# A streaming encoder step on one core: stationary tiles low in SBUF, and the up projection with tokens on partitions

## The chip, the cores and the metric

The kernel runs on one core of a Trainium2 chip. The metric is the device time of one execution in microseconds (us), less being better. The work is in float32, with every large product made of three products of a high and a low part.

## The reference

One layer of a hybrid encoder, for 256 prompt tokens and 8 x 16 sample tokens, 384 in all, with the same weights.

```python
h    = rmsnorm(x, norm_mix_g)                 # x: 384 tokens x 2048
proj = h @ w_in                               # GLU in | q | k | v | forget logits | gate A | gate B
u    = glu(proj); z = layernorm(causal_dwconv(u, 31 taps))
a    = swish(z) @ conv_pw_out
b    = forgetting_attention(q, k, v, logf, caches) @ w_att_out
x    = x + (sigmoid(gA) * a + sigmoid(gB) * b) @ w_out
h2   = rmsnorm(x, norm_ffn_g)
up   = h2 @ w_up                              # 2048 x 11264: gate half g, linear half u
gc   = causal_dwconv(g, 3 taps over time)     # per channel, per stream
x    = x + (silu(gc) * u) @ w_down            # 5632 x 2048
```

It returns x and the new caches and states (k, v, forget logits, conv rows, the last two gate rows).

## The kernel before

**Three products.** A weight block of 256 rows x 512 columns (two steps k of 128) arrives by one DMA of 512 KB as tile raw. ScalarE casts it to hi (line 144, type float32r), VectorE subtracts hi from raw to get lo (line 145). There are three raw buffers and two hi/lo pairs. Activations are kept as high and low parts too: tiles of 2 x 4 x 384 elements a partition (12,288 bytes), channels on partitions, tokens along the row. Each step k then takes three matmuls: high by high, high by low, low by high.

**Two kinds of job.** The function gemm runs jobs of nk steps. In kind "A" the weight block is stationary (128 x 128) and the 384 tokens move, lines 235 to 237; there are four blocks m, so 12 matmuls a step, and the result has channels on partitions. In kind "B" the activation is stationary (128 tokens at a time, three blocks t) and 512 weight columns move, lines 240 to 242; 9 matmuls a step, tokens on partitions. A job gathers in 4 or 3 of the five banks of the pool acc. At its last step evac empties each bank and done starts what follows. Before each pair of steps, ahead(2) gives out fetch and split of further weight pairs, until two are ready.

**Order.** PE, in parts SP, ScalarE and VectorE follow the order of the program; for the rest a planner works out, before the launch, the order on each engine from priorities (splits and evacuations are given out as if 150 and 60 instructions earlier) and from its own table of durations. after(n, f) runs f after n further steps.

**Stages.** V (columns 344 wide, kind B) with the first norm: first_norm transposes x by chunks on TensorE, x_chunk multiplies by the norm weight and splits into hT, lines 272 to 276. Then K, Q (B); GLU (A) beside attention; the gates (B, evacuated on ScalarE with a sigmoid, line 759) beside the 31-tap conv on VectorE; attention out with aHL and pointwise out with zt stationary (B, 8 steps each); w_out with mix (B). The second norm: x_chunk2 makes xg, second_norm gets 1/rms per token as a column, and diagonals and over_partitions (a product with ones, line 322) spread it as rs2 along the row of every partition. Then the feed-forward part: 11 groups of 512 channels, each with one up job for g and one for u (both A, 16 steps), and three rounds of down jobs (B, stationary act) after groups 4, 8 and 10.

In a group, up_g_evac multiplies PSUM by rs2 on VectorE into extf (line 939; 24 blocks of 16 tokens, each with two columns of left context, filled by POOL, lines 941 and 942). up_g_done runs the three taps on VectorE (956, 958), Silu on ScalarE (960) and sg = silu * rs2 on POOL (961). up_u_evac multiplies PSUM by sg (978) and splits into act (980, 981).

**Places in SBUF.** 229,376 bytes a partition are there. The lowest 16,384 are the descriptor scratch of POOL's DMAs. From the left follow the constants, raw, hi, lo, and five slots of 12,288 bytes for hT, mix, act and ut. From the right come attT, the conv tiles, attention's aHL, zt, the gates, and later y and xg. By the sizes of the tiles, in bytes from the start of a partition:

| tile | before | after |
|---|---|---|
| hi | 33,888 to 42,080 | 2,176 to 14,464 |
| lo | 42,080 to 50,272 | 211,968 to 224,256 |
| five act slots | 50,272 to 111,712 | 14,464 to 75,904 |
| aHL0, aHL1 | 178,432 to 203,008 | 75,904 to 100,480 |
| zt0 | 166,144 to 178,432 | 100,480 to 112,768 |
| zt1 | 217,056 to 229,344 | 112,768 to 125,056 |
| xg0 to xg3 | 178,592 to 227,744 | 75,904 to 125,056 |

Of the kernel before, what the change touches and what calls it, by code (L numbers as in the profile page):

```python
# [40 lines left out]
def hybrid_step(  # L41
# [20 lines left out]

    cp, close_cp = pool("consts")
    wp, close_wp = pool("weights")
    gp, close_gp = pool("acts")
# [58 lines left out]
    def stream_tile():  # L124
        return wp.tile([P, 2, 512], F32, tag="raw", bufs=3, name="raw")

# [90 lines left out]
    def gemm(jobs, sides=()):  # L217
        for js in jobs:
            js = js if isinstance(js, tuple) else (js,)
            for j in js:  # L220
                nb = 4 if j["kind"] == "A" else NTT
                j["ps"] = [(misc_tile if j is not js[0] and i == 2 else acc_tile)() for i in range(nb)]
            for j, k in [(j, k + i) for k in range(0, js[0]["nk"], 2) for j in js for i in range(2)]:
                nb, n, nk, ps = len(j["ps"]), j["n"], j["nk"], j["ps"]
                kk = k % 2
                if kk == 0:
                    ahead(2)
                    hi, lo = ready.pop(0)
                ah, al = j["act"](k)
                st, sp = k == 0, k == nk - 1  # L230
                for m in range(nb):
                    s = slice(m * P, (m + 1) * P)
                    if j["kind"] == "A":
                        o = ps[m][:, :NT]
                        mm(o, hi[:, kk, s], ah, start=st, stop=False)  # L235
                        mm(o, hi[:, kk, s], al, start=False, stop=False)  # L236
                        mm(o, lo[:, kk, s], ah, start=False, stop=sp)  # L237
                    else:
                        o = ps[m][:, :n]
                        mm(o, ah[:, s], hi[:, kk, :n], start=st, stop=False)  # L240
                        mm(o, ah[:, s], lo[:, kk, :n], start=False, stop=False)  # L241
                        mm(o, al[:, s], hi[:, kk, :n], start=False, stop=sp)  # L242
# [69 lines left out]

    def diagonals(p, r, tag):
        dg = p.tile([P, NTT, P], F32, tag=tag + "d", name=tag + "d")
# [61 lines left out]
    def first_norm():  # L376
        for c in range(2, 16, 2):
            yield
            x_chunk(c)
            yield  # L380
            x_chunk(c + 1)
            yield
            if c % 4 == 2:
# [13 lines left out]
        yield  # L397
        dg = diagonals(p_x0, rs1, "r1")
        yield
# [363 lines left out]
    def layer_norm():  # L763
# [24 lines left out]
        yield  # L788
        dg = diagonals(p_cv, rv, "rv")
        yield  # L790
# [3 lines left out]
        for c in range(8):  # L794
# [8 lines left out]
            yield  # L803

    zt = [p_z.tile([P, 2, 4, NT], F32R, name="zt0"), p_t.tile([P, 2, 4, NT], F32R, tag="T", name="zt1")]

# [47 lines left out]
    def open_resid():  # L854
        close_sg()
        close_z()
        close_hl()
        close_cv()
        close_t()
        p_r, res["close_r"] = pool("resid", side="right")  # L860
        res["y"] = y = p_r.tile([P, NTT, DM], F32, name="y")
        res["xg"] = [p_r.tile([P, 2, 4, NT], F32R, name=f"xg{g}") for g in range(4)]
        res["rs2"] = p_r.tile([P, NT], F32, name="rs2")
        res["ss2"] = p_r.tile([P, NTT, 4], F32, name="ss2")
# [34 lines left out]
    def second_norm():  # L899
# [15 lines left out]
    for u, i0 in enumerate(range(0, 11, 3)):  # L915
# [11 lines left out]
        after(2 + 2 * u, ffn_state)  # L927
    extf = [p_f.tile([P, 24, 18], F32, name=f"extf{m}") for m in range(4)]
    for m in range(4):
        nc.gpsimd.memset(extf[m][:, 0, 0:2], 0.0)  # L930
    xa = grouped(xg)
    acts = {}

    def up_g_evac(g, sg):
        def ev(m, ps):
            c = 4 * g + m
            e = extf[m]
            v = e[:, :, 2:18]
            tt(v, ps[:, :NT].rearrange("p (a t) -> p a t", t=16), rs2[:].rearrange("p (a t) -> p a t", t=16),
               op=ALU.mult)  # L940
            nc.gpsimd.tensor_copy(e[:, 1:16, 0:2], e[:, 0:15, 16:18])
            nc.gpsimd.tensor_copy(e[:, 16:24, 0:2], sfT[:, c, :].rearrange("p (b r) -> p b r", r=2))
        return ev

    def up_g_done(g, sg):
        def done():
            gcs = [p_f.tile([P, NT], F32, tag="gc", bufs=4, name="gc") for _ in range(4)]
            lc = p_f.tile([P, 18, 4], F32, tag="lc", bufs=2, name="lc")
            for w in range(3):
                for m in range(4):  # L950
                    c = 4 * g + m
                    o = gcs[m][:].rearrange("p (a t) -> p a t", t=16)
                    v = extf[m][:, :, w:w + 16]
                    wc = fw[:, w * 44 + c:w * 44 + c + 1]
# [4 lines left out]
            for m in range(4):  # L959
                nc.scalar.activation(gcs[m][:], gcs[m][:], AF.Silu)  # L960
                nc.gpsimd.tensor_tensor(sg[m][:], gcs[m][:], rs2[:], op=ALU.mult)
                nc.gpsimd.tensor_copy(lc[:, :, m].rearrange("p (a r) -> p a r", r=2), extf[m][:, 15:24, 16:18])

# [10 lines left out]

    def up_u_evac(g, sg):
        def ev(m, ps):
            a = p_f.tile([P, NT], F32, tag="ac", bufs=2, name="ac")
            tt(a[:], ps[:, :NT], sg[m][:], op=ALU.mult)
            hi, lo = acts[g][:, 0, m, :], acts[g][:, 1, m, :]
            nc.scalar.copy(hi, a[:])  # L980
            tt(lo, a[:], f(hi), op=ALU.subtract)
# [25 lines left out]
    close_f()  # L1007
    close_r()
    close_misc()
    close_acc()  # L1010
    close_gp()
    close_wp()
    close_cp()
    close_dr()
# [33 lines left out]
```

## Time and profile before

| what | value |
|---|---|
| median of 3 runs | 2037.92 us (2037.69 to 2038.57) |
| profiled execution, its own time | 2039.01 us |
| its span, first to last instruction | 2037.3 us |
| TensorE, busy | 2028.7 us |
| VectorE, busy | 1030.2 us |
| ScalarE, busy | 712.6 us |
| POOL, busy | 161.4 us |
| DMA | 276.12 MB, mean 136 GB/s |

A line of the groups reads: line, engine, operation, tiles written <- tiles read (the moving one ahead of the stationary one for matmuls), shape, count, then busy us in all, mean ns of one, and idle us of the engine just before, with what ended that idle time. Matmuls overlap in the pipeline, so their listed durations add up to more than the span. A timeline row begins with the start and the length in us. A row of the waits names who waited for whom, us in all, how often, and the longest. A row of the chain of waits has start, length and what ran.

### The profile page before, as it was taken

The page shows a single profiled execution, that of the slowest core. Times are in us where ns is not written, and L with a number is a line of the kernel's source. Part 1 is how long each engine was busy: PE and PEld are TensorE (multiplying, and loading weights), DVE is VectorE, ACT ScalarE, POOL GpSimd, SP SyncE. Part 2 cuts the span into 40 slices and gives each one's busy share as a digit, 9 for nine tenths or more (in the row PEclk, how much of TensorE's full clock was granted, in tenths as well). Part 3 has the DMA queues.
Part 4 walks back from the last instruction along what each step waited for, and adds up shares of the span by engine and source line. Part 5 has one row for each costly group of instructions (what it writes and reads, how often), then busy time and mean ns, then how long its engine had stood idle before and what let it go on. Part 6 is the DMA issues. An engine that isn't in the chain of part 4 may idle for free.

```text
span 2037.3 us, 26618 instructions
## 1 busy us (share of the span) xinstructions
PE 2028.7 (100%) x10668; PEld 1835.8 (90%) x10668; DVE 1030.2 (51%) x1416; ACT 712.6 (35%) x1034; POOL 161.4 (8%) x258
## 2 busy tenths in 40 slices
PE   9999999999999999999999999999999999999999
PEld 9988999988888888889999999889999998899987
DVE  4434477788753645344545354333544453335443
ACT  5444555433333523333323232322322332223322
POOL 2000011000000000000222022000221120002100
PEclk9999999999999999999999999999999999999999
DMA  6555555444444343643444444444444444444453
GB/s 181 170 169 158 152 169 152 117 133 134 134 129 130 121 123 118 193 124 114 125 127 124 134 125 125 133 125 132 128 124 125 130 130 125 130 128 126 128 152 124
DMA packets 175749, 276.12 MB, mean 136 GB/s; under 512 B 11998, under 2 KB 63217, under 8 KB 175617
## 3 DMA queue, kind: packets, MB, share of 16 engines
q1 hardware_dynamic: 175305, 273.84, 45.1%
q8 instruction: 83, 1.36, 0.3%
q0 software_dynamic: 288, 0.57, 0.2%
q14 instruction: 41, 0.34, 0.1%
q10 hardware_dynamic: 32, 0.01, 0.0%
HBM read 266.98 MB, written 7.86 MB: 135 GB/s over the span
## 4 chain that ended last, share of the span: by engine, by line
PE 98%; DVE 1%; DMA 0%; ACT 0%; issue 0%; SPq 0%; ACTq 0%; DVEq 0%
PE acc L241 17%; PE acc L242 17%; PE acc L240 17%; PE acc L235 14%; PE acc L236 14%; PE acc L237 14%; DMA xs<-in_x_sample_dram 0%; PE misc L559 0%; PE misc L885 0%; PE misc L838 0%; PE misc L272 0%; PE misc L625 0%; PE misc L592 0%; DVE lo L145 0%; PE misc L611 0%
## 5 line engine op out<-in xcount | busy, mean ns | idle before, releaser
L145 DVE TENSOR_TENSOR lo<-raw,hi 128x1024 fp32r<-128x1024 f32 (+2 forms) x481 | 585.2, 1217 | 907.5 <-ACT hi L144 902.3
L144 ACT CAST hi<-raw 128x1024 fp32r<-128x1024 f32 (+2 forms) x481 | 498.2, 1036 | 1169.1 <-PE acc L242 642.5
L235 PE MATMUL acc<-xg,hi 128*128 128x384 f32 x1408 | 474.9, 337 | 0.0
L237 PE MATMUL acc<-xg,lo 128*128 128x384 f32 x1408 | 473.1, 336 | 0.0
L236 PE MATMUL acc<-xg,hi 128*128 128x384 f32 x1408 | 473.1, 336 | 0.0
L240 PE MATMUL acc<-hi,hT 128*128 128x512 f32 (+1 forms) x704 | 267.6, 380 | 0.0
L241 PE MATMUL acc<-lo,hT 128*128 128x512 f32 (+1 forms) x704 | 265.3, 377 | 0.9 <-DVE lo L145 0.9
L235 PEld LDWEIGHTS acc<-xg,hi 128*128 128x128 f32 x1408 | 264.7, 188 | 1.4
L242 PE MATMUL acc<-hi,hT 128*128 128x512 f32 (+1 forms) x704 | 265.3, 377 | 0.0
L236 PEld LDWEIGHTS acc<-xg,hi 128*128 128x128 f32 x1408 | 264.8, 188 | 0.1
L237 PEld LDWEIGHTS acc<-xg,lo 128*128 128x128 f32 x1408 | 264.7, 188 | 0.0
L241 PE MATMUL acc<-lo,act 128*128 128x512 f32 x528 | 205.4, 389 | 0.0
L242 PE MATMUL acc<-hi,act 128*128 128x512 f32 x528 | 205.4, 389 | 0.0
L240 PE MATMUL acc<-hi,act 128*128 128x512 f32 x528 | 205.4, 389 | 0.0
L711 DVE SCALAR_TENSOR_TENSOR ut<-ext,cw,ut 128x384 f32<-128x384 f32 x240 | 152.1, 634 | 6.2
L241 PEld LDWEIGHTS acc<-lo,hT 128*128 128x128 f32 x704 | 132.5, 188 | 23.6 <-DVE lo L145 1.6
L240 PEld LDWEIGHTS acc<-hi,hT 128*128 128x128 f32 x704 | 132.5, 188 | 22.5 <-issue 0.2
L242 PEld LDWEIGHTS acc<-hi,hT 128*128 128x128 f32 x704 | 132.3, 188 | 22.6
L242 PEld LDWEIGHTS acc<-hi,act 128*128 128x128 f32 x528 | 99.1, 188 | 20.8
L241 PEld LDWEIGHTS acc<-lo,act 128*128 128x128 f32 x528 | 99.1, 188 | 20.4
L240 PEld LDWEIGHTS acc<-hi,act 128*128 128x128 f32 x528 | 99.1, 188 | 20.4
L235 PE MATMUL acc<-hT,hi 128*128 128x384 f32 x256 | 90.0, 352 | 0.0
(292 smaller groups left out, 1941.6 us busy)
## 6 DMA issues: line engine op xcount, KB each, us to landing
raw<-in_w_up_dram SPq DMA_DIRECT2D x176, 512.0 KB, 3.6
raw<-in_w_in_dram SPq DMA_DIRECT2D x96, 512.0 KB, 3.5
raw<-in_w_down_dram SPq DMA_DIRECT2D x88, 512.0 KB, 3.7
raw<-in_w_in_dram SPq DMA_DIRECT2D x64, 256.0 KB, 2.9
raw<-in_w_out_dram SPq DMA_DIRECT2D x32, 512.0 KB, 3.6
raw<-in_w_att_out_dram SPq DMA_DIRECT2D x16, 512.0 KB, 3.7
raw<-in_conv_pw_out_dram SPq DMA_DIRECT2D x16, 512.0 KB, 3.7
raw<-in_w_in_dram SPq DMA_DIRECT2D x23, 344.0 KB, 3.1
```

The lines of the kernel that those rows point to most:

```text
L144: nc.scalar.copy(hi[:, k, :o], raw[:, k, :o])
L145: tt(lo[:, k, :o], raw[:, k, :o], f(hi[:, k, :o]), op=ALU.subtract)
L235: mm(o, hi[:, kk, s], ah, start=st, stop=False)
L236: mm(o, hi[:, kk, s], al, start=False, stop=False)
L237: mm(o, lo[:, kk, s], ah, start=False, stop=sp)
L240: mm(o, ah[:, s], hi[:, kk, :n], start=st, stop=False)
L241: mm(o, ah[:, s], lo[:, kk, :n], start=False, stop=False)
L242: mm(o, al[:, s], hi[:, kk, :n], start=False, stop=sp)
L711: stt(o, v, wc, o, op0=ALU.mult, op1=ALU.add)
```

## The change

The constants, raw and lo go to the right side, hi to the bottom of the left; aHL, zt and xg go to the left behind the act slots; the descriptor scratch shrinks to 2,048 bytes. There are three hi/lo pairs and ahead(3). In first_norm each pair of chunks is turned one step later. The up jobs become kind B: ScalarE evacuates with the token's 1/rms as scale into tok (tokens on partitions), and VectorE turns it back by 16 transposes of 32 partitions x 384 elements a job, into extf or uT. The spread of rs2 goes, and POOL's product with it. The product of u with sg reads SBUF now.

```diff
-    cp, close_cp = pool("consts")
-    wp, close_wp = pool("weights")
+    cp, close_cp = pool("consts", side="right")
+    rp, close_rp = pool("raw_lo", side="right")
+    wp, close_wp = pool("hi")
...
-        return [wp.tile([P, 2, 512], F32R, tag=tag, bufs=2, name=tag) for tag in ("hi", "lo")]
+        return [p.tile([P, 2, 512], F32R, tag=tag, bufs=3, name=tag) for p, tag in ((wp, "hi"), (rp, "lo"))]
...
-                    ahead(2)
+                    ahead(3)
...
         for c in range(2, 16, 2):
             yield
+            yield
             x_chunk(c)
             yield
             x_chunk(c + 1)
-            yield
...
-    p_hl, close_hl = pool("attHL", side="right")
+    p_hl, close_hl = pool("attHL")
     aHL = [p_hl.tile([P, 2, 4, NT], F32R, name=f"aHL{i}") for i in range(2)]
-    p_z, close_z = pool("z", side="right")
+    zt = [p_hl.tile([P, 2, 4, NT], F32R, name=f"zt{i}") for i in range(2)]
...
+        p_xg, res["close_xg"] = pool("xg")
+        res["xg"] = [p_xg.tile([P, 2, 4, NT], F32R, name=f"xg{g}") for g in range(4)]
...
-        res["rs2"] = p_r.tile([P, NT], F32, name="rs2")
+        res["rs2"] = p_r.tile([P, NTT], F32, name="rs2")
...
-        dg = diagonals(p_f, r2, "r2")
-        after(2, lambda: over_partitions(dg, rs2[:]))
+        nc.vector.tensor_copy(rs2[:], r2[:])
...
-    def up_g_evac(g, sg):
-        def ev(m, ps):
-            c = 4 * g + m
-            e = extf[m]
-            v = e[:, :, 2:18]
-            tt(v, ps[:, :NT].rearrange("p (a t) -> p a t", t=16), rs2[:].rearrange("p (a t) -> p a t", t=16),
-               op=ALU.mult)
-            nc.gpsimd.tensor_copy(e[:, 1:16, 0:2], e[:, 0:15, 16:18])
-            nc.gpsimd.tensor_copy(e[:, 16:24, 0:2], sfT[:, c, :].rearrange("p (b r) -> p b r", r=2))
+    def tok_rows():
+        return p_f.tile([P, NTT, 512], F32, tag="tok", bufs=1, name="tok")
+
+    def up_evac(rows):
+        def ev(t, ps):
+            nc.scalar.activation(rows[:, t, :], ps[:], AF.Identity, scale=rs2[:, t:t + 1])
         return ev
 
-    def up_g_done(g, sg):
+    def blocks(rows, put):
+        src = rows[:].rearrange("p t (m b j) -> p b m t j", m=4, b=4)
+        for b in range(4):
+            for a in range(4):
+                nc.vector.transpose(put(a, slice(32 * b, 32 * b + 32)), src[32 * a:32 * a + 32, b])
+
+    def up_g_done(g, rows, sg):
         def done():
+            def put(a, js):
+                return extf[js].rearrange("p m (t a) c -> p m t a c", t=NTT)[:, :, :, 2 * a:2 * a + 2, 2:18]
+
+            blocks(rows, put)
...
             for m in range(4):
-                nc.scalar.activation(gcs[m][:], gcs[m][:], AF.Silu)
-                nc.gpsimd.tensor_tensor(sg[m][:], gcs[m][:], rs2[:], op=ALU.mult)
+                nc.scalar.activation(sg[m][:], gcs[m][:], AF.Silu)
...
-    def up_u_evac(g, sg):
-        def ev(m, ps):
-            a = p_f.tile([P, NT], F32, tag="ac", bufs=2, name="ac")
-            tt(a[:], ps[:, :NT], sg[m][:], op=ALU.mult)
-            hi, lo = acts[g][:, 0, m, :], acts[g][:, 1, m, :]
-            nc.scalar.copy(hi, a[:])
-            tt(lo, a[:], f(hi), op=ALU.subtract)
-        return ev
+    def up_u_done(g, rows, sg):
+        def done():
+            uT = p_f.tile([P, 4, NT], F32, tag="uT", bufs=1, name="uT")
+            blocks(rows, lambda a, js: uT[js].rearrange("p m (t a i) -> p m t a i", t=NTT, a=4)[:, :, :, a])
+            for m in range(4):
+                tt(uT[:, m], uT[:, m], sg[m][:], op=ALU.mult)
+                hi, lo = acts[g][:, 0, m, :], acts[g][:, 1, m, :]
+                nc.scalar.copy(hi, uT[:, m])
+                tt(lo, uT[:, m], f(hi), op=ALU.subtract)
+        return done
...
-        return [job("A", 16, xa, up_g_evac(g, sg), done=up_g_done(g, sg)), job("A", 16, xa, up_u_evac(g, sg))]
+        gr, ur = tok_rows(), tok_rows()
+        return [job("B", 16, xa, up_evac(gr), done=up_g_done(g, gr, sg)),
+                job("B", 16, xa, up_evac(ur), done=up_u_done(g, ur, sg))]
...
-    nc = _bacc.Bacc("TRN2", target_bir_lowering=False, num_devices=1)
+    nc = _bacc.Bacc("TRN2", target_bir_lowering=False, num_devices=1, dynamic_dma_scratch_size=2048)
```

More of the change, by code (lines that the diff above doesn't have):

```diff
@@ L124, in stream_tile @@
     def stream_tile():
-        return wp.tile([P, 2, 512], F32, tag="raw", bufs=3, name="raw")
+        return rp.tile([P, 2, 512], F32, tag="raw", bufs=3, name="raw")
     def fetch_row(raw, srcs, k):
@@ L311, in hybrid_step, with diagonals @@
     rs1b = cp.tile([P, NT], F32, name="rs1b")
-    def diagonals(p, r, tag):
-        dg = p.tile([P, NTT, P], F32, tag=tag + "d", name=tag + "d")
+    def diagonals(dg, r):
         for t in range(NTT):
@@ L397, in first_norm @@
         yield
-        dg = diagonals(p_x0, rs1, "r1")
+        dg = diagonals(p_x0.tile([P, NTT, P], F32, name="r1d"), rs1)
         yield
@@ L803, in layer_norm @@
             yield
-    zt = [p_z.tile([P, 2, 4, NT], F32R, name="zt0"), p_t.tile([P, 2, 4, NT], F32R, tag="T", name="zt1")]
     def conv_branch():
@@ L855, in open_resid @@
         close_sg()
-        close_z()
-        close_hl()
         close_cv()
         close_t()
+        close_hl()
+        p_xg, res["close_xg"] = pool("xg")
+        res["xg"] = [p_xg.tile([P, 2, 4, NT], F32R, name=f"xg{g}") for g in range(4)]
         p_r, res["close_r"] = pool("resid", side="right")
         res["y"] = y = p_r.tile([P, NTT, DM], F32, name="y")
-        res["xg"] = [p_r.tile([P, 2, 4, NT], F32R, name=f"xg{g}") for g in range(4)]
-        res["rs2"] = p_r.tile([P, NT], F32, name="rs2")
+        res["rs2"] = p_r.tile([P, NTT], F32, name="rs2")
         res["ss2"] = p_r.tile([P, NTT, 4], F32, name="ss2")
@@ L952, in done @@
                     o = gcs[m][:].rearrange("p (a t) -> p a t", t=16)
-                    v = extf[m][:, :, w:w + 16]
+                    v = extf[:, m, :, w:w + 16]
                     wc = fw[:, w * 44 + c:w * 44 + c + 1]
@@ L1008, in hybrid_step @@
     close_r()
+    res["close_xg"]()
     close_misc()
@@ L1012, in hybrid_step @@
     close_wp()
+    close_rp()
     close_cp()
```

14 lines of the change are left out of this document (9 added, 5 removed).

## The prediction

> **What bounds the kernel now.** I read the page first (busy times, the chain of waits, the groups), then single rows of the timeline, because a mean in the groups is the length of one pipelined matmul and not the distance to the next.
>
> ```profile
> span 2037.3 us, 26618 instructions
> PE 2028.7 (100%) x10668; PEld 1835.8 (90%) x10668; DVE 1030.2 (51%) x1416; ACT 712.6 (35%) x1034; POOL 161.4 (8%) x258
> PE 98%; DVE 1%; DMA 0%; ACT 0%; issue 0%; SPq 0%; ACTq 0%; DVEq 0%
> L235 PE MATMUL acc<-xg,hi 128*128 128x384 f32 x1408 | 474.9, 337 | 0.0
> L236 PE MATMUL acc<-xg,hi 128*128 128x384 f32 x1408 | 473.1, 336 | 0.0
> L237 PE MATMUL acc<-xg,lo 128*128 128x384 f32 x1408 | 473.1, 336 | 0.0
> ACT hi L144 <- PE acc L236: 473.9, 170, 3.5
> ```
>
> TensorE is busy for 2028.7 of 2037.3 us and holds 98% of the chain that ends last. ScalarE's casts wait for TensorE, not the other way round. So time is the sum over matmuls of the distance from one start to the next; a change pays only by fewer matmuls, a shorter distance, or fewer pauses. The up projection is 3 x 1408 = 4224 matmuls with 384 columns, of lines 235 to 237. Their listed 337 ns cannot be the distance: 4224 x 337 ns would be 1423 us of overlapping bars. The distances come from pairs of timeline rows. Between the first and the second row of each pair below lie 60 starts (30 for zt):
>
> ```profile
> 1009.90 0.34 PE L236 MATMUL acc<-xg,hi 128*128 128x384 f32 x1
> 1020.30 0.34 PE L236 MATMUL acc<-xg,hi 128*128 128x384 f32 x1
> 149.76 0.39 PE L240 MATMUL acc<-hi,hT 128*128 128x512 f32 x1
> 163.36 0.39 PE L240 MATMUL acc<-hi,hT 128*128 128x512 f32 x1
> 1289.97 0.39 PE L242 MATMUL acc<-hi,act 128*128 128x512 f32 x1
> 1303.57 0.39 PE L242 MATMUL acc<-hi,act 128*128 128x512 f32 x1
> 664.90 0.39 PE L240 MATMUL acc<-hi,aHL 128*128 128x512 f32 x1
> 678.90 0.39 PE L240 MATMUL acc<-hi,aHL 128*128 128x512 f32 x1
> 738.01 0.40 PE L240 MATMUL acc<-hi,zt 128*128 128x512 f32 x1
> 745.01 0.40 PE L240 MATMUL acc<-hi,zt 128*128 128x512 f32 x1
> ```
>
> Up projection, 384 columns: 10.40 us / 60 = 173.3 ns. 512 columns with hT or act stationary: 13.60 / 60 = 226.7 ns. 512 columns with aHL stationary: 14.00 / 60 = 233.3 ns; the two zt rows, 30 starts apart, give 7.00 / 30, the same. The slope between the first two is (226.7 - 173.3) / 128 = 0.417 ns a column, so 384 columns cost 160.0 ns and 512 cost 213.3 ns, and **every matmul pays 13.3 ns on top, but 20.0 ns with aHL or zt stationary**. The page's row of granted clocks is at nine tenths or more in every slice, 1.00 in the windows below.
>
> What separates 13.3 from 20.0? By the tile sizes of the code, the stationaries that pay 13.3 ns lie between byte 33,888 (hi, in the up projection) and 111,712 (end of the fifth act slot) of a partition; zt and aHL lie at 166,144 and above. The moving side does not matter: in the up projection xg moves from 178,592 and above and still pays 13.3. I read this as a step in the address of the stationary somewhere between 111,712 and 166,144.
>
> **The change part by part.**
>
> *Up projection turned over.* It goes from 4224 x 173.33 ns = 732.2 us to 11 groups x 2 jobs x 16 x 3 x 3 = 3168 matmuls of 512 columns. The multiplied columns are the same (1.62 million); 1056 fixed parts fall away. xg, now stationary, moves to 75,904 to 125,056: xg0, xg1 and nearly all of xg2 inside the range measured at 13.3 ns, xg3 (112,768 to 125,056) in the unmeasured gap. At 226.67 ns the stage takes 718.1 us, **-14.1 us**. If xg3 paid 20.0: 792 x 6.67 ns = 5.3 us less gain. I take the low value: xg3 begins 1 KB past the measured range and ends 40 KB short of the first tile that pays more.
>
> *aHL and zt low.*
>
> ```profile
> L242 PE MATMUL acc<-hi,aHL 128*128 128x512 f32 x96 | 38.2, 398 | 0.0
> L241 PE MATMUL acc<-lo,zt 128*128 128x512 f32 x96 | 37.9, 395 | 0.0
> L237 PE MATMUL acc<-hT,lo 128*128 128x384 f32 x256 | 85.9, 336 | 0.0
> 964.89 0.67 PE misc L322 x6
> ```
>
> 3 lines x 96 for each of the two, 576 matmuls at 6.67 ns less: **-3.8 us** (zt1 lies where xg3 does; without it -2.9). Against that, lo goes to the right side, to about 212,000, and in the GLU jobs it is stationary (line 237, 256 matmuls): **+1.7 us**. The ones and avg tiles go up too, but serve fewer than 20 matmuls. The six-piece product that spread rs2 over partitions goes with line 322's second use: **-0.7 us**, on TensorE and so on the path.
>
> *Evacuation.* PSUM is now emptied by three ScalarE activations a job instead of four VectorE products, and VectorE turns blocks. The last two rows are stretches: length, then busy time (and count) of TensorE, weight loads, VectorE, ScalarE, POOL, then the granted clock.
>
> ```profile
> L759 ACT ACTIVATE sgA<-acc,rs 128x512 f32<-128x512 f32 x12 | 8.2, 686 | 6.7 <-PE acc L242 6.7
> L144 ACT CAST hi<-raw 128x1024 fp32r<-128x1024 f32 (+2 forms) x481 | 498.2, 1036 | 1169.1 <-PE acc L242 642.5 <-PE acc L236 473.9 <-issue 28.0
> L145 DVE TENSOR_TENSOR lo<-raw,hi 128x1024 fp32r<-128x1024 f32 (+2 forms) x481 | 585.2, 1217 | 907.5 <-ACT hi L144 902.3 <-DMA bs<-c_dr 4.7
> L939 DVE TENSOR_TENSOR extf<-acc,rs 128x384 f32<-128x384 f32 x44 | 23.3, 557 | 5.1 <-PE acc L237 5.1
> L981 DVE TENSOR_TENSOR act<-ac,act 128x384 fp32r<-128x384 f32 x44 | 24.1, 556 | 7.0 <-ACT act L980 6.4
> L632 DVE COPY attT<-misc 128x256 f32<-128x256 f32 x8 | 3.4, 421 | 1.4 <-PE misc L631 1.4
> L577 DVE COPY kT<-misc 128x384 f32<-128x384 f32 x8 | 4.4, 553 | 12.2 <-PE misc L576 12.2
> L958 DVE SCALAR_TENSOR_TENSOR gc<-extf,fw,gc 128x384 f32<-128x384 f32 x88 | 56.0, 697 | 0.0
> 1073.00:1206.00 133.00, 133.00 (x770) 132.79 (x769) 64.93 (x81) 41.70 (x50) 22.23 (x32) 1.00 0.44 128
> 500.00:640.00 140.00, 140.00 (x623) 115.93 (x622) 85.19 (x110) 46.23 (x56) 4.00 (x5) 1.00 0.45 132
> ```
>
> ScalarE: 3 x 0.69 = 2.1 us a job, the form of line 759. The accumulators are 5 banks; a job takes 3, so the next job's third tile needs the first tile's bank. That is 6 matmuls (1.4 us) into the next job, and the first tile is complete 6 matmuls before its own job ends: 2.7 us for an activation of 0.69, even behind one cast of 1.04. The gate stage works just so (three banks, line 759), and there TensorE was busy for all 140.00 us with VectorE busy for 85.19. Taken at 0.
>
> VectorE: per group 32 transposes of 32 x 384 elements come in and four evacuations (4 x 0.557 = 2.2 us) go. No row shows a transpose. The two copies of 256 and 384 elements took 421 and 553 ns, so 1.03 ns an element and 157 ns fixed; one pass of 384 is 0.55 us, the strided three-operand row (697 ns) is the upper neighbour, and two passes would be 157 + 2 x 396 = 949 ns. I take 0.6, near the copies, as it has one input too. The Trainium skill ("VectorE: DVE Perf Modes", The three transpose paths) gives 311 ns for a 128 x 128 bf16 block transpose; scaled by three that is an estimate of 0.93 us, no run here shows it, and it would leave the sum as it is. Now the load: the row from 1073 us covers two groups, 64.93 us of VectorE, 32.5 each. After: 32.5 - 2.2 + 32 x 0.6 = 49.5 us in a group that TensorE holds for 2 x 144 x 226.67 ns = 65.3 us, 76%; at 0.95 us a transpose, 93%. The cover is TensorE; it fails when a transpose costs (65.3 - 30.3) / 32 = 1.09 us. Behind the transposes wait only the taps and the Silu, whose result sg is first read a whole job (32.6 us) later. Of the u halves only act10 is wanted soon: the last down jobs read it from k = 8, 72 matmuls or 16.3 us in, and its first quarter needs the evacuation (2.1), 16 transposes (9.6), two products (1.1) and two weight splits between them (2.4): 15.2 us. 0, with +3 at worst.
>
> *One tok buffer.* The u evacuation on ScalarE waits for the transposes of the g half, and behind it wait the weight casts. Those transposes were given out a job earlier and need about 10 us of VectorE plus splits; 0.
>
> *Third hi/lo pair.* A split may now start two weight pairs (2 x 18 x 226.67 ns = 8.2 us) ahead and not one.
>
> ```profile
> 398.89 1.23 DVE lo L145
> 400.16 0.50 PE acc L241
> L241 PE MATMUL acc<-lo,hT 128*128 128x512 f32 (+1 forms) x704 | 265.3, 377 | 0.9 <-DVE lo L145 0.9
> 11.82 0.33 PE L272 MATMUL misc<-ident,xs 128*128 128x128 f32 x1 [0.70 <-DMA xs<-in_x_sample_dram]
> 43.34 0.49 PE L272 MATMUL misc<-ident,xs 128*128 128x128 f32 x3
> 44.21 0.57 ACT L275 ACTIVATE hT<-misc,gm 128x384 fp32r<-128x384 f32 x1
> 45.13 0.61 DVE L276 SCALAR_TENSOR_TENSOR hT<-misc,gm,hT 128x384 fp32r<-128x384 f32 x1
> L961 POOL TENSOR_TENSOR sg<-gc,rs 128x384 f32<-128x384 f32 x44 | 59.9, 1389 | 12.7 <-ACT gc L960 12.7
> ```
>
> Waits for lo cost TensorE 0.9 us in all, for instance at 400 us: **-0.5 us**. More important, the pair covers VectorE's new bursts: a split takes 1.04 + 1.22 us, so lo may come 5.9 us late, and a single transpose delays it by 0.6.
>
> *Start.* first_norm turns each pair of x chunks one tick later. A chunk took from 43.34 to 45.74 us, 2.4 us, from its transposes to its low part. One tick is 9 matmuls of about 158 ns, 1.4 us, so the first chunk of a pair now has 0.33 + 1.4 + 0.33 and the low part 0.3 more, about 2.4: just enough, with up to 0.5 us lost per pair, seven times. The 0.7 us wait for x at 11.82 should go. Taken at 0, between -0.7 and +3.5.
>
> *No cost.* The POOL product of line 961 (59.9 us) goes, but nobody on the path waited for it. The DMAs of the weights, their number and order on SP's queue are the same. The smaller descriptor scratch serves only POOL's few early loads.
>
> Sum: -14.1 - 3.8 + 1.7 - 0.7 - 0.5 = **-17.4 us**, so the profiled span goes from 2037.3 to 2019.9. The profiled execution took 2039.01 us, the median of the runs is 2037.92; I take the difference off the median: **2020.5 us**. Its own range, from start, tail and pauses: 2018 to 2026. What a measurement here can tell from no change is about 0.2%, 4 us.
>
> **The rivals.**
>
> 1. *xg3 and zt1 lie above the step.* +5.3 + 1.0: 2026.8 us. The gap where the step can lie is 53 KB wide and these tiles reach 13 KB into it, which by length alone would be 25%; the one round address in the gap is 131,072, above them, and the range measured flat contains the round 65,536. 9%.
>
> 2. *The address is not what costs 6.7 ns.* It could be what these two stages share, eight-step jobs on other weights; then aHL, zt and lo stay as they are: 2020.5 + 3.8 - 1.7 = 2022.6. For it: aHL and zt are the only witnesses. Against it: act jobs are on another weight too, and pay 13.3. 5%. The Trainium skill ("SBUF — State Buffer", Who interferes with whom) says that TensorE's read ports wait for no other engine and names no dependence on the address within a partition; this rival is what follows from it. A worse form: xg pays 20.0 wherever it lies, 3168 x 233.33 = 739.2 us, 2020.5 + 21.1 = 2041.6. 3%.
>
> 3. *VectorE becomes the bound (slower).* Place: the up groups. It decides from 1.09 us a transpose; at 1.3 us a group takes 30.3 + 41.6 = 71.9 us, 6.6 more than TensorE, eleven times: +73, 2093 us. For it: the operation is unmeasured here, it reads in runs of 32 and writes in runs of 16 with a shift of partitions. Against it: even two passes come to 0.95. 6%.
>
> 4. *Hand-over stalls.* The evacuations sit on ScalarE behind a cast that itself waits for TensorE, or splits fall behind a burst; 0.6 us at each of the 22 jobs is +13: 2033.5. For it: the order on the engines is fixed ahead of time from durations that were not measured here. Against it: the gate stage. 8%.
>
> 5. *The lowest tiles are cheaper still.* Slots 0 and 1 of the act pool move to 14,464 to 39,040, most of it below what is measured; a further 6.7 ns less for half of the 3 x 704 matmuls with hT is -7: 2013.5, and with act and mix as much again. 2%.
>
> **How the numbers follow.** The forecast has 67%. Range 2016.5 to 2031.0: it holds the forecast's own range, rivals 1 and 2 without its worse half, and the milder part of 4; left out are 3, 5, that half and the rest of 4, some 15%. Faster by over 0.2% (below 2033.8): forecast, 1, 2, 5 and over half of 4, 0.88. Within: the worse half of 2 and part of 4, 0.04. Slower: 3 and the rest, 0.08.
>
> **What would show it.** 226.7 ns between starts in the up groups, 680 ns for three with aHL and zt, 233 ns for line 237's GLU matmuls; a transpose row of 0.5 to 0.7 us and VectorE near 75% in the up groups; TensorE without pauses at job boundaries. I am wrong if xg steps at 233.3, if the transpose is above 1.09 us, or if TensorE's idle time before L240 names ScalarE or VectorE.

## The result and the profile after

The changed kernel takes 2067.36 us (median of 4 runs, 2065.19 to 2069.14), the kernel before 2037.97 in the same session: a ratio of 1.0143, 95% interval 1.0126 to 1.0161. The forecast was 2020.5. The profiled execution of the changed kernel took 2065.19 us, its span is 2063.4.

The head of the page after, and the shares of the chain that ended last:

```profile
span 2063.4 us, 24707 instructions
PE 2051.4 (99%) x9606; PEld 1700.8 (82%) x9606; DVE 1189.5 (58%) x1722; ACT 755.7 (37%) x1099; POOL 97.3 (5%) x214
PE 97%; DVE 1%; ACT 1%; DMA 0%; issue 0%; SPq 0%; ACTq 0%
```

TensorE is busy for nearly the whole span, as before (99%, then 100%), holds the chain as before (97%, then 98%), and runs 1062 matmuls fewer; yet it is busy 22.7 us longer, while its idle time grew by only 3.4 us (8.6 to 12.0). So in the main neither a wait nor another engine took the gain: the matmuls themselves follow one another more slowly. The timeline of TensorE after, with pairs of rows 60 starts apart (30 for aHL), shows it; columns are start, length, what ran:

```profile
1299.68 0.39 PE L242 MATMUL acc<-lo,act 128*128 128x512 f32 x1
1313.55 0.39 PE L242 MATMUL acc<-lo,act 128*128 128x512 f32 x1
1494.62 0.39 PE L242 MATMUL acc<-lo,xg 128*128 128x512 f32 x1
1508.48 0.39 PE L242 MATMUL acc<-lo,xg 128*128 128x512 f32 x1
744.79 0.39 PE L243 MATMUL acc<-hi,zt 128*128 128x512 f32 x1
758.65 0.39 PE L243 MATMUL acc<-hi,zt 128*128 128x512 f32 x1
689.77 0.40 PE L241 MATMUL acc<-hi,aHL 128*128 128x512 f32 x1
696.77 0.40 PE L241 MATMUL acc<-hi,aHL 128*128 128x512 f32 x1
```

Down jobs (act): 13.87 / 60 = 231.2 ns, where before had 226.7. Up jobs (xg): 13.86 / 60, the same 231. zt: 231.0; aHL 7.00 / 30 = 233.3. For the three matmuls of one step and token block that is 693 to 700 ns in place of 680, in **every** stage of kind B, also in those the change did not touch. In the GLU jobs (kind A) three take 526.7 ns in place of 520.

What the change brought to the other engines is near the forecast. Groups (VectorE's transposes, ScalarE's evacuation), then the waits of TensorE's matmuls (who waited, for whom: us in all, times, longest):

```profile
L943 DVE STREAM_TRANSPOSE uT<-tok 32x384 f32<-32x384 f32 x176 | 100.2, 570 | 2.6
L936 ACT ACTIVATE tok<-acc,rs 128x512 f32<-128x512 f32 x66 | 45.3, 686 | 37.9 <-PE acc L243 37.7
```

```profile
PE acc L243 <- DVE hT L277: 1.8, 7, 0.4
PE acc L241 <- ACT vt L413: 1.7, 2, 1.3
PE acc L241 <- ACT hT L276: 1.2, 1, 1.2
PE acc L243 <- DVE act L990: 0.2, 1, 0.2
```

A transpose takes 0.57 us, an evacuation 0.69, and nothing in the up groups makes TensorE wait. But the first three of these waits are new. All lie in the V stage, where first_norm makes hT. The stretch from 7 to 107 us, before and after (columns as in the prediction: length, busy time and count of TensorE, weight loads, VectorE, ScalarE, POOL, granted clock, DMA):

```profile
7.00:107.00 100.00, 98.91 (x593) 93.14 (x592) 43.58 (x82) 48.50 (x86) 4.52 (x14) 1.00 0.60 176
```

```profile
7.00:107.00 100.00, 95.26 (x557) 89.03 (x556) 43.17 (x79) 47.47 (x82) 3.93 (x14) 0.98 0.57 167
```

593 matmuls before, 557 after. From V's first matmul to K's first the trace shows 75.8 us before and 83.1 after: 7.3 us lost, half of it (98.91 - 95.26) in TensorE's longer pauses.

The lengths of the stages, each unbroken stretch of one kind counted from the start of its first matmul to the start of its last, add the two losses up (the last three columns belong to experiments below):

| matmuls by tile, us | before | after | e1 | e9 | e12 |
|---|---|---|---|---|---|
| V, K and Q (hT) | 208.3 | 218.1 | 218.3 | 217.7 | 208.9 |
| GLU (hT) | 179.3 | 180.2 | 179.7 | 179.4 | 179.4 |
| gates (hT) | 263.9 | 269.0 | 263.2 | 263.3 | 263.3 |
| aHL, zt | 139.8 | 139.2 | 136.7 | 136.7 | 136.7 |
| mix | 136.3 | 138.5 | 136.3 | 136.3 | 136.3 |
| up (xg) | 737.0 | 737.9 | 722.6 | 722.7 | 722.7 |
| down (act) | 358.4 | 365.9 | 359.2 | 359.2 | 359.2 |

### The profile page after: what moved, and what is told of

Same layout as the page of the kernel before. It is cut to its first block, busy times and chain, and to the rows that moved or that the text cites. A ratio compares the mean times of both kernels' runs of the same rounds, so it can differ in the third digit from the quotient of the medians.

```text
span 2063.4 us, 24707 instructions
## 1 busy us (share of the span) xinstructions
PE 2051.4 (99%) x9606; PEld 1700.8 (82%) x9606; DVE 1189.5 (58%) x1722; ACT 755.7 (37%) x1099; POOL 97.3 (5%) x214
## 4 chain that ended last, share of the span: by engine, by line
PE 97%; DVE 1%; ACT 1%; DMA 0%; issue 0%; SPq 0%; ACTq 0%
PE acc L243 29%; PE acc L241 29%; PE acc L242 29%; PE acc L236 2%; PE acc L238 2%; PE acc L237 2%; DVE lo L146 0%; DMA raw<-in_w_in_dram 0%; ACT hi L145 0%; DVE uT L943 0%; PE misc L559 0%; PE misc L836 0%; PE misc L883 0%; PE misc L625 0%; PE misc L592 0%
## 5 line engine op out<-in xcount | busy, mean ns | idle before, releaser
L241 PE MATMUL acc<-hi,xg 128*128 128x512 f32 x1056 | 418.3, 396 | 0.0
L243 PE MATMUL acc<-hi,xg 128*128 128x512 f32 x1056 | 416.0, 394 | 0.0
L242 PE MATMUL acc<-lo,xg 128*128 128x512 f32 x1056 | 414.8, 393 | 0.0
L241 PE MATMUL acc<-hi,hT 128*128 128x512 f32 (+1 forms) x704 | 271.3, 385 | 2.9 <-ACT vt L413 1.7
L243 PE MATMUL acc<-hi,hT 128*128 128x512 f32 (+1 forms) x704 | 269.3, 383 | 1.8 <-DVE hT L277 1.8
L243 PEld LDWEIGHTS acc<-hi,xg 128*128 128x128 f32 x1056 | 198.3, 188 | 47.0
L241 PEld LDWEIGHTS acc<-hi,xg 128*128 128x128 f32 x1056 | 198.2, 188 | 46.5
L242 PEld LDWEIGHTS acc<-lo,xg 128*128 128x128 f32 x1056 | 198.5, 188 | 45.4
L243 PE MATMUL acc<-hi,act 128*128 128x512 f32 x528 | 208.5, 395 | 0.2 <-DVE act L990 0.2
L241 PE MATMUL acc<-hi,act 128*128 128x512 f32 x528 | 207.8, 394 | 0.0
L243 PEld LDWEIGHTS acc<-hi,hT 128*128 128x128 f32 x704 | 132.9, 189 | 29.4 <-DVE hT L277 3.8
L943 DVE STREAM_TRANSPOSE uT<-tok 32x384 f32<-32x384 f32 x176 | 100.2, 570 | 2.6
```

The costliest lines, as they stand in the source:

```text
L943: nc.vector.transpose(put(a, slice(32 * b, 32 * b + 32)), src[32 * a:32 * a + 32, b])
```

## The experiments

All ratios are against the kernel before, run on the same chip in the same session (its median there 2038.3 to 2038.7). Differences between two experiments of different sessions carry that shift and the spread of the runs, which was largest in e9, 2027.62 to 2031.69 us. Two theories on the longer step were tested. The place theory: what costs is how high a tile lies in a partition. The offset theory: what costs is that the stationary tile and the moving one start at different remainders of some power of two of bytes. The expectations of e1 to e4 split the place theory into SIDES (the mover changes between low and high) and HIGH MOVER (the mover lies high), and set beside it ALIGNMENT (starts at multiples of 128 bytes cost) and THIRD PAIR; the offset theory is named from e9 on. The tile sizes give these remainders of 256 bytes, known only by the end; every block that these matmuls read within a tile lies a multiple of 256 bytes from the tile's start:

| kernel, stage | stationary | hi | lo | three matmuls, ns |
|---|---|---|---|---|
| before: hT, mix, act | 96 | 96 | 96 | 680 |
| before: aHL, zt0; zt1 | 0; 224 | 96 | 96 | 700 |
| changed: all of kind B | 128 | 128 | 0 | 693 to 700 |
| e1, e9, e10: all of kind B | 128 | 128 | 128 | 680 |
| e2: all of kind B | 128 | 0 | 0 | some 697 |
| e3: act, mix | 96 | 96 | 224 | 693, 700 |
| e4: aHL, zt | 96 | 96 | 96 | 680 |
| e8: aHL, zt | 0 | 96 | 96 | 700 |
| e11: aHL0, aHL1 | 128, 160 | 96 | 96 | 700, 700 |
| e11: zt0 | 96 | 96 | 96 | 680 |
| e11: zt1 | 32 | 96 | 96 | 687 |

**e1, lo on the left.** The changed kernel with lo in hi's pool:

```diff
-        return [p.tile(... bufs=3 ...) for p, tag in ((wp, "hi"), (rp, "lo"))]
+        return [p.tile(... bufs=3 ...) for p, tag in ((wp, "hi"), (wp, "lo"))]
```

> The changed kernel with lo back on the left side (14,464 to 26,752), so hi and lo both move from low places; three pairs and every tile still at a multiple of 128 bytes. The changed kernel takes 693.3 or 700 ns for three 512-column matmuls instead of 680. Theory SIDES (a moving operand that changes between a low and a high place costs 6.7 ns at each change, 13.3 a triple): 680 ns in hT, mix, act and xg, 520 in the GLU jobs; 2624 triples of 512 columns x some 14 ns less = -37 us, GLU -1.7, xg3's low half now above 131,072 at most +1.8: 2029 to 2031 us. Theory HIGH MOVER (lo costs 13.3 ns because it moves from a high place): the same. Theory ALIGNMENT (a start at a multiple of 128 bytes, where the kernel before had 96 past one, costs it): stays at 693 to 700, 2067 us. Theory THIRD PAIR: stays, 2067 us.

2031.92 us, ratio 0.9963 (0.995 to 0.9976): 35.4 us less than the changed kernel with lo moved, and the act slots and the tiles behind them 12,288 bytes (a multiple of 256) further up. The timeline, 60 starts apart as above:

```profile
1299.67 0.39 PE L243 MATMUL acc<-hi,act 128*128 128x512 f32 x1
1313.27 0.39 PE L243 MATMUL acc<-hi,act 128*128 128x512 f32 x1
1494.73 0.39 PE L242 MATMUL acc<-lo,xg 128*128 128x512 f32 x1
1508.33 0.39 PE L242 MATMUL acc<-lo,xg 128*128 128x512 f32 x1
```

13.60 / 60 = 226.7 ns for act and xg. With that step the turned up projection is 14.4 us shorter than before (722.6 against 737.0). ALIGNMENT and THIRD PAIR are out, as every start is still a multiple of 128 bytes and there are still three pairs. lo, the moving tile, sets the step: the prediction had only priced it as a stationary.

**e2, hi on the right too.**

```diff
-        return [... for p, tag in ((wp, "hi"), (rp, "lo"))]
+        return [... for p, tag in ((rp, "hi"), (rp, "lo"))]
```

> The changed kernel with hi on the right side as well, so both moving parts come from high places and none changes sides. SIDES: 680 ns a triple in all 512-column stages (-37 us), GLU with all three stationaries high 540 ns (+3.4 us against 526.7): about 2034 us. HIGH MOVER: each of the three movers costs 13.3, 720 ns a triple, 2624 x 26 = +68 us: about 2135 us. ALIGNMENT and THIRD PAIR: 693 to 700 stays, GLU 540, about 2070 us.

2073.03, ratio 1.0169 (1.0152 to 1.0186). The stretch from 1300 to 1400 us, inside the first round of down jobs, columns as above:

```profile
1300.00:1400.00 100.00, 100.00 (x432) 81.06 (x431) 45.06 (x51) 27.24 (x28) 0.00 (x0) 1.00 0.36 127
```

432 matmuls, where the changed kernel has 435 (under e9): three take some 697 ns. SIDES (2034) and HIGH MOVER (2135) both missed. Two displaced movers cost hardly more than one, so the cost isn't paid per displaced tile.

**e3, the kernel before with lo on the right.**

```diff
+    lp_, close_lp = pool("lo_r", side="right")
...
-        return [wp.tile(...) for tag in ("hi", "lo")]
+        return [p.tile(...) for p, tag in ((wp, "hi"), (lp_, "lo"))]
```

> The kernel before with one edit: lo to the top of the right side (221,152), two pairs, starts still 96 past a multiple of 128. SIDES and HIGH MOVER: 693.3 in place of 680 ns in the hT, mix and act stages (about 1376 triples x 13.3 = +18.3 us), and lo as a high stationary +6.7 ns in 256 GLU and 1408 up triples (+11.1 us): about 2067 us. ALIGNMENT and THIRD PAIR: the stages with hT, mix and act stay at 680; only the stationary lo costs 11.1 us: 2049 us; if the place of the stationary costs nothing either, 2038 us.

2066.25, ratio 1.0136 (1.0121 to 1.0152): this one move in the old kernel costs 28 us, nearly as much as the changed kernel lost (29.4). The 2067 us expected of SIDES and HIGH MOVER came out, though e2 had spoken against both: lo's start has another remainder here too (table).

**e4, the kernel before with aHL and zt on the left** (at 97,376 to 146,528, and the smaller descriptor scratch to make room):

```diff
-    p_hl, close_hl = pool("attHL", side="right")
+    p_hl, close_hl = pool("attHL")
...
+    zt = [p_hl.tile([P, 2, 4, NT], F32R, name=f"zt{i}") for i in range(2)]
```

> The kernel before with aHL and zt on the left (aHL0 97,376, aHL1 109,664, zt0 121,952, zt1 134,240 to 146,528), descriptor scratch 2,048, else the same. If the place of the stationary sets their 700 ns a triple: aHL0 and aHL1 (below 121,952) 680, and within zt0 and zt1 a step to 700, at 131,072 if it is a round address; about -2.5 to -3.8 us: 2034 to 2035.5 us. If the place of the stationary does not matter: 700 everywhere, 2038 us.

2035.23, ratio 0.9986 (0.9976 to 0.9995), 3.1 us less. aHL0 in the second job, zt1 in the first:

```profile
675.99 0.39 PE L240 MATMUL acc<-hi,aHL 128*128 128x512 f32 x1
682.78 0.39 PE L240 MATMUL acc<-hi,aHL 128*128 128x512 f32 x1
734.94 0.39 PE L240 MATMUL acc<-hi,zt 128*128 128x512 f32 x1
741.74 0.39 PE L240 MATMUL acc<-hi,zt 128*128 128x512 f32 x1
```

6.79 and 6.80 / 30 = 226.7 ns, for zt1 too, which ends at 146,528. Up to here the offset theory holds, and so does a place theory that doesn't count the displaced tiles.

**e5, e6, e7: the start and the third pair,** all with lo on the left. e5 puts first_norm's old order back, e6 has two hi/lo pairs, e7 both:

```diff
         for c in range(2, 16, 2):
             yield
-            yield
             x_chunk(c)
             yield
             x_chunk(c + 1)
+            yield
```

```diff
-        return [... bufs=3 ...]
+        return [... bufs=2 ...]
...
-                    ahead(3)
+                    ahead(2)
```

> The kernel with lo on the left (2031.9 us, three pairs), with the one later step of the x chunks taken back. Its first 1008 matmuls (V, K, Q) take 218.3 us against 208.3 in the kernel before. Theory TICK (x chunks come one step too late: seven pauses of 0.55 us for the low part of hT and pauses of 1.6 and 0.7 us for the V evacuation that waits for the later end of the norm): those go, about -5 us, 2027 us, and the pause of 3.5 us near 13 us with the slow clock after it stays. Theory PAIR (the third pair's cast stands on ScalarE ahead of the x chunk's activation and waits there for its weights): the 3.5 us pause and the slow clock stay, and with them most of the loss, 2030 to 2032 us. If both are one chain, the stretch goes back to 208.3: 2022 us.

> The kernel with lo on the left, with two hi/lo pairs in place of three (and two split ahead), x chunks still one step later. PAIR: the 3.5 us pause near 13 us and the slow clock after it go, about -6 us: 2026 us, the seven pauses stay. TICK: about 2031. If instead the third pair is what covers VectorE's bursts of transposes in the up groups, TensorE waits for lo there: 0.5 us or more in each of 22 jobs, 2035 us or more.

> The kernel with lo on the left, two pairs and the x chunks as in the kernel before: of the change only the places of the tiles and the up projection turned over remain. TICK and PAIR together: the first stretch goes back to 208.3 us, -10: 2021 to 2022 us, close to the 2020.5 of the forecast; the pauses for lo that were seen before (0.9 us) stay. If the third pair is needed for VectorE's bursts: 2030 us or more.

e5: 2021.77, ratio 0.9919 (0.9905 to 0.9932). e6: 2047.33, ratio 1.0042 (1.0029 to 1.0055). e7: 2041.28, ratio 1.0013 (1.0004 to 1.0022). e5 came out as its last branch has it (one chain, 2022), e6 and e7 as theirs on VectorE's bursts (2035 or more, 2030 or more). The old order is worth 10.1 us with three pairs (e1 to e5) and 6.0 with two (e6 to e7); the third pair is worth 19.5 (e7 to e5). The waits of TensorE's matmuls and weight loads in e7:

```profile
PE acc L242 <- DVE lo L146: 7.7, 13, 0.9
PEld acc L242 <- DVE lo L146: 26.3, 47, 1.3
```

and the longest up stretch in e7 and then in e5:

```profile
932.00:1263.00 331.00, 327.43 (x1434) 264.22 (x1433) 226.29 (x340) 124.28 (x158) 25.74 (x64) 1.00 0.39 125
```

```profile
932.00:1263.00 331.00, 331.00 (x1471) 272.49 (x1470) 228.84 (x341) 127.79 (x163) 29.72 (x64) 1.00 0.40 128
```

With two pairs TensorE's line 242 stands still for lo 7.7 us, and the weight loads 26.3, where the kernel before lost 0.9 with two pairs and no transposes on VectorE; in this stretch 1434 matmuls get done, not 1471. In e5 no wait for lo is left. How the new order hurts is seen in the timeline of the changed kernel (all engines) from the transposes of a pair of chunks on:

```profile
13.83 0.49 PE L273 MATMUL misc<-ident,xs 128*128 128x128 f32 x3
14.27 0.77 ACT L145 CAST hi<-raw 128x688 fp32r<-128x688 f32 x1 [1.26 <-DMA raw<-in_w_in_dram]
14.94 0.57 ACT L276 ACTIVATE hT<-misc,gm 128x384 fp32r<-128x384 f32 x1
15.56 0.43 PE L241 MATMUL acc<-hi,hT 128*128 128x344 f32 x1 [1.24 <-ACT hT L276]
15.86 0.61 DVE L277 SCALAR_TENSOR_TENSOR hT<-misc,gm,hT 128x384 fp32r<-128x384 f32 x1
16.52 0.42 PE L243 MATMUL acc<-hi,hT 128*128 128x344 f32 x1 [0.37 <-DVE hT L277]
```

The transposes are issued at 13.83, right before the matmuls that need them; a weight cast, which itself waited for its weights until 14.27, stands before ScalarE's L276, and TensorE idles 1.24 us for the high part, then 0.37 for the low part. A wait for the low part, 0.23 to 0.25 us, comes back at each of the six later pairs (the seven waits for L277 above). In e1 the weights of the same cast came later:

```profile
15.66 0.77 ACT L145 CAST hi<-raw 128x688 fp32r<-128x688 f32 x1 [1.31 <-DMA raw<-in_w_in_dram]
```

There TensorE's pause for L276 was 3.26 us (last section). In both kernels TensorE goes on 1.3 us after that cast's start (at 15.56 and 16.96), so what the new order costs here depends on when the weights land. In the kernel before, L275 of this pair ran at 13.32, right behind one cast and ahead of the next.

**e8, the place against the offset.** The kernel before with aHL and zt between 129,280 and 178,432, the first of them where e4 had put zt:

```diff
+    sgA = ...
     p_hl, close_hl = pool("attHL", side="right")
     aHL = [...]
+    zt = [p_hl.tile([P, 2, 4, NT], F32R, name=f"zt{i}") for i in range(2)]
+    sgB = ...
```

> The kernel before with aHL and zt at 129,280 to 178,432 (aHL0 from 129,280, aHL1 from 141,568, zt0 from 153,856, zt1 from 166,144), hi and lo low. Up to 146,528 a stationary was seen to cost no more (680 ns a triple), from 166,144 it was seen at 700. If a place in between is the step, aHL0 stays at 680 and the step shows in aHL1 or within zt0, whose four steps lie 1,536 bytes apart: zt1 700. If it is not the place but the pool or the order in which the tiles lie, all four come out alike.

One run of 2038.81 us. aHL0 in the second job, zt0 in the first:

```profile
676.57 0.39 PE L240 MATMUL acc<-hi,aHL 128*128 128x512 f32 x1
683.57 0.39 PE L240 MATMUL acc<-hi,aHL 128*128 128x512 f32 x1
728.68 0.39 PE L240 MATMUL acc<-hi,zt 128*128 128x512 f32 x1
735.68 0.39 PE L240 MATMUL acc<-hi,zt 128*128 128x512 f32 x1
```

7.00 / 30 = 233.3 ns from the first step, although aHL0 now starts at 129,280, 4,960 bytes *below* zt1's start in e4, which ran at 226.7. No threshold of place fits both.

**e9, the offset alone.** The changed kernel, lo still on the right, with 384 unused bytes in a constant, so that lo starts at 211,584 in place of 211,968:

```diff
-    fw = cp.tile([P, 3 * 44], F32, name="fw")
+    fw = cp.tile([P, 3 * 44 + 96], F32, name="fw")
```

> The changed kernel with one edit: a constant tile 384 bytes longer, which shifts lo from 211,968 to 211,584; lo stays on the right and high. The starts of hi, act, aHL, zt and xg leave 128 when divided by 512, lo left 0 and leaves 128 now. Theory OFFSET (what counts is whether stationary and moving tiles start at the same remainder of 512 bytes; their place high or low does not matter): 680 ns a triple in all 512-column stages, 520 in GLU, 2067 - 35 = about 2030 to 2033 us, the late start remaining. Theory PLACE (lo costs because it lies high): 693 to 700 stays, 2067 us.

2029.64, ratio 0.9956 (0.9941 to 0.997): 37.7 us less than the changed kernel. The pad also shifts raw and every tile that is opened later on the right side; none of these is read by the large products. The stretch from 1300 to 1400 us in the changed kernel and in e9:

```profile
1300.00:1400.00 100.00, 100.00 (x435) 81.26 (x434) 44.00 (x50) 27.14 (x28) 0.00 (x0) 1.00 0.39 128
```

```profile
1300.00:1400.00 100.00, 100.00 (x443) 82.81 (x442) 35.56 (x33) 26.17 (x25) 0.00 (x0) 1.00 0.39 131
```

435 matmuls and 443 in the same 100 us, at the same clock. The place of lo does nothing; its start decides.

**e10, the period.** e5 with lo shifted by 256 bytes more against hi and act, to tell a period of 512 from one of 256 (the expectation counts remainders of 512):

```diff
+    q1, close_q1 = pool("pad1")      # one unused tile of 256 bytes in each of q1 and q2
+    lp_, close_lp = pool("lo")
+    q2, close_q2 = pool("pad2")
...
-        return [... for p, tag in ((wp, "hi"), (rp, "lo"))]
+        return [... for p, tag in ((wp, "hi"), (lp_, "lo"))]
```

> The 2021.8 us kernel (lo low, three pairs, old ticks) with 256 unused bytes before and after lo: all tiles low as there, but lo's start leaves 384 of 512 where all others leave 128. OFFSET: 693 to 700 ns a triple and 526.7 in GLU again, +30 to +37 us: 2052 to 2059 us. PLACE: 2022 us, 680.

2021.99, ratio 0.9918 (0.9904 to 0.9933). I had expected the loss to come back, and nothing happened (443 matmuls from 1300 to 1400 us, as in e9): 256 bytes are the period, or it divides them.

**e11, four offsets.** e4 with the starts of aHL0, aHL1, zt0, zt1 shifted by +32, +64, +256 and -64 bytes against hi and lo:

```diff
-    aHL = [p_hl.tile([P, 2, 4, NT], F32R, ...)]; zt = [...]
+    aHL = [moved("aHL0", 32), moved("aHL1", 32)]     # 32 unused bytes ahead of each
+    zt = [moved("zt0", 192), moved("zt1", 192)]      # 192 unused bytes ahead of each
```

> The kernel before with aHL and zt on the left (2035.2 us, all at 680 ns), now each starting at another remainder than hi and lo: aHL0 +32 bytes, aHL1 +64, zt0 +256, zt1 -64. OFFSET: those offsets that are no whole period of the memory's interleaving take 700 ns; if the period is 512 bytes all four do; if it is 32 or 64 bytes, aHL0 or aHL1 on stay at 680; zt0 tells 256 from 512. PLACE: 680 in all.

One run of 2037.0 us. aHL1, zt0 and zt1, first job:

```profile
667.68 0.40 PE L240 MATMUL acc<-hi,aHL 128*128 128x512 f32 x1
674.69 0.39 PE L240 MATMUL acc<-hi,aHL 128*128 128x512 f32 x1
728.18 0.39 PE L240 MATMUL acc<-hi,zt 128*128 128x512 f32 x1
734.99 0.39 PE L240 MATMUL acc<-hi,zt 128*128 128x512 f32 x1
736.35 0.39 PE L240 MATMUL acc<-hi,zt 128*128 128x512 f32 x1
743.22 0.39 PE L240 MATMUL acc<-hi,zt 128*128 128x512 f32 x1
```

7.01, 6.81 and 6.87 / 30: +64 costs the full 6.7 ns a matmul (aHL0's +32 as well, table), +256 nothing, -64 a third of it. So +32 and +64 here, and 128 in the changed kernel, rule out those shorter periods: equal remainders of 256 bytes are free, and of those tried with 512 moving columns no other is.

**e12, both mends.** The changed kernel with e9's padding and e5's order:

> The changed kernel with both small edits: 384 unused bytes in the constants, so that lo starts at the same remainder of 256 bytes as every activation tile while it stays on the right side, and the old order in the first norm. Theory (the remainder of 256 bytes, and the start's order, are the whole loss and add up): 2029.6 less the 10.1 us that the old order gave between the two kernels with lo on the left, so 2019.5, within 2018 to 2023; V, K and Q near 207.6 us in all, all triples 680 ns. Rival (lo on the left helps by its place as well): 2024 or more, with K, Q or the up stages longer than with lo on the left. Rival (the old order gains only where lo is on the left): near 2029.6.

2022.2 (2021.55 to 2022.41), ratio 0.9918 (0.9905 to 0.9932): 45.2 us less than the changed kernel, by 384 unused bytes and the place of a yield. The order gave 7.4 us over e9, less than the 10.1 expected; the runs of e1 and e9 spread over 3 to 4 us, so the two figures can hardly be told apart. It equals e5 within 0.5 us, so lo's side makes no difference that these runs can tell. Both beat the kernel before and the changed one.

## Why the prediction was wrong

The miss is 2067.4 - 2020.5 = 46.9 us, and it comes apart into three: lo's start against the other tiles, 37.7 (after to e9); first_norm's order, 7.4 (e9 to e12); what is left between e12 and the forecast, 1.7.

*The step that failed* is the reading of 13.3 and 20.0 ns as a step in the stationary's address, with "the moving side does not matter". The rows were read rightly, and e4 shows that the aHL and zt tiles do lose 3 us as forecast when they move; but they gained because their start came to the same remainder as hi and lo, not because it came low. A wrong cause gave the right size there, by luck, and the wrong sign elsewhere: lo was priced at +1.7, as stationary in the GLU jobs, while as moving tile against act, hT, mix, xg it cost some 37. The evidence for "the moving side does not matter" was xg moving from 178,592 in kind A with 384 columns at no cost; it did not carry over to 512 columns. The tile table of before allowed the other reading: it gives remainders of 96 for hi, lo and act and 0, 0, 224 for aHL, zt0, zt1. I compared addresses by size only. But xg, at 160 against 96 and without cost, would have spoken against it too. One of the signs named was wrong by the prediction's own numbers: line 237 in GLU moves 384 columns, so 6.7 ns more makes 180.0 and not 233 ns; three matmuls took 526.7, as 173.3 + 173.3 + 180.0 gives.

*Rival 2* (the address is not what costs) named the doubt, and its worse half, 2041.6, had the mechanism nearest to the truth: xg paying more wherever it lies. It had no price for hT, mix and act. The Trainium skill ("SBUF — State Buffer", Who interferes with whom) lists TensorE's port for the moving tile and the one for the weight load as independent; e9 against the changed kernel, 435 and 443 matmuls in 100 us by a shift of lo by 384 bytes, does not fit a full independence, if it is these two reads that meet. That they meet is inferred; the runs show only the dependence on both starts.

*The start* was the second term that failed: taken at 0 with +3.5 at worst, it cost 7.4 to 10.1. The chain of 2.4 us against 2.4 us was worked out as "just enough" without the weight cast that stands before ScalarE's step and waits for its DMA, and without what a pause brings behind it (last section).

*Third pair*: put at -0.5 for the waits it removes. The forecast said that it covers VectorE's bursts, without a price for the cover; that price is 19.5 us. The sum was not wrong by it, since the pair was part of the change, but the turned up projection alone would have lost what it gains: e7, without the pair, is at 1.0013.

*Right*: the up projection at -14.1 (measured 722.6 - 737.0 = -14.4 with equal starts); the size of aHL and zt, -3.8 (e4: -3.1), not its cause; a transpose at 0.6 us (0.570), so VectorE not the bound with three pairs; evacuation on ScalarE at 0 (no wait of TensorE for it in the tables); the act10 tail near 0 (0.5 us waited at L990 in e5). With equal starts and the old order, 2022.2 and 2021.8 stand against 2020.5.

## What to carry to other kernels

For float32r products like these, place tiles so that a matmul's stationary and moving operands start at the same remainder of 256 bytes, and check this again whenever a pool, a constant or a scratch size moves: here 384 bytes in an unrelated tile were worth more than the whole rewrite. When every matmul of a stage takes some ns more and no engine waits, busy shares and the chain say nothing; count matmuls per 100 us, or the distance of starts, in a stage the change left alone. And when bursts of work go to the engine that feeds TensorE, buy the buffer that covers them in the same change, and leave the chain that feeds the first matmuls as early as it was.

## What the hardware showed that I had not expected

For 512 moving columns the mean distance for three matmuls takes a few values, 680, 687, 693 and 700 ns, steps of about 6.7; only e2, where both movers are displaced, lies between them at 697. At mixed starts (the changed kernel) it stays at 693 or 700 for long stretches and switches at interruptions, such as a transpose between the jobs. Why is open. So is why some narrower movers pay nothing. The sign of the difference, stationary less moving, matters: in e11 +64 cost 20 ns for three at 512 columns and -64 (zt1) only 7. In the kernel before, the up projection moved 384 columns of xg (remainder 160) against hi and lo (96), also -64, at 520 ns for three, no cost at all. Narrowness alone isn't the reason: with lo at 224 (+64) the same up jobs took 526.7 in e3, and so did the GLU jobs of the changed kernel (lo 128 away from hT). Only five unequal differences (32, 64, 128, 160, 192) were tried, and no run separated the weight load's read from the matmul's.

After a pause TensorE can run at half pace for a while. In e1's timeline:

```profile
16.96 0.65 PE L241 MATMUL acc<-hi,hT 128*128 128x344 f32 x1 [3.26 <-ACT hT L276]
22.38 0.49 PE L243 MATMUL acc<-hi,hT 128*128 128x344 f32 x1
22.67 0.49 PE L241 MATMUL acc<-hi,hT 128*128 128x344 f32 x1
```

After the idle time of 3.26 us the matmuls of 344 columns follow one another at 287 ns (22.38 to 22.67) until 23.2 us, and then at 158: some 22 of them, 3 us in all on top of the pause. The Trainium skill ("TensorE: Matmul & The Clock Gate", Why this matters for your kernels) says that pauses over about 3 us bring the clock down to half, and this row agrees; in the changed kernel a spell of eleven such matmuls came at 66.6 us after pauses of only 1.32 and 0.36 us, which that rule alone doesn't give. In e1 the granted clock was 0.83 in the stretch from 7 to 27 us, and 1.00 in the same stretch of the kernel before. Such a spell makes the price of a late start larger than its waits. It may also make it different from run to run, as the landing of the weights does; that was not tested.
